# A macaron transformer block on one core: the engines' queues ordered by the scheduler's time-line machine

## The chip, the cores and the metric

The kernel runs on one core of a Trainium2 chip. Its time is that of the device in microseconds (us), given as the median over several runs. A core has a matrix engine (TensorE, PE in the profile), whose weight loads are listed apart (PEld), a vector engine (VectorE, DVE), a scalar engine (ScalarE, ACT), GpSimd (POOL) and SyncE (SP), which here issues nearly all DMAs. Each engine works through its own queue of instructions in a fixed order. An instruction waits at the head of its queue for semaphores that other engines or DMAs raise, and everything behind it on that engine waits with it.

## The reference

One layer on x of shape (1, 1024, 1024) with a condition c, all in float32:

```
h = x + 0.5 * g1 * postRMS(SwiGLU_1(mod1(preRMS(x))))
h = h + g2 * postRMS(Mixer(mod2(preRMS(h))))
h = h + 0.5 * g3 * postRMS(SwiGLU_2(mod3(preRMS(h))))

SwiGLU(u) = (silu(u @ w_gate) * (u @ w_up)) @ w_down      # 1024 -> 2816 -> 1024
stick-breaking (8 heads of 64): w[t,s] = sigmoid(z) * prod over s<j<t of sigmoid(-z[t,j]), s < t;  out = w @ v
differential (4 heads): (softmax(q1 k1 + bias) - lam * softmax(q2 k2 + bias)) @ v, normalised
Mixer = (sigmoid(ga) * (ya @ w_branch_sb) + sigmoid(gd) * (yd @ w_branch_da)) @ w_out
```

The scale and shift of mod1 to mod3 and the gates g1 to g3 come from c by a matrix-vector product with w_ada (adaLN): nine vectors of 1024 numbers.

## The kernel before

**Products.** A float32 product is made of three float32r products of 128 x 128 by 512 columns: each operand is split into a high half H (a cast, mostly on ScalarE: L141, L225, L960) and a low half L (a subtraction, mostly on VectorE: L142, L226, L961), and H x H, L x H and H x L are summed in one PSUM bank. Weights and activations come in as 128 x 1024 or 128 x 512 blocks over SP's queue (raw, raw2, stg), are split into wsH and wsL (or sbH, sbL, tbH, tbL), and TensorE works on them.

**Stages in order.** The *start*: the first adaLN vectors and the normalised, transposed and split input (uH, uL). *FFN 1, first part*: 11 pairs of gate and up matrices by a Strassen-like scheme (L298 to L300: blocks u, T1 to T4, B22, with weight sums s21 and s34 made on VectorE, L331 to L336; bank evictions into q on ScalarE and VectorE, L352 to L404). Between the pairs, the generator `steps` makes the adaLN vectors that later stages need, some instructions at a time: `mod_acc` (L82 to L91) loads a block of w_ada (wada, 512 KB, L87) and adds it to macc on VectorE, eight times per vector, in tiles of the tag "row", of which there are four; L101 and L125 bring macc through TensorE, and L126 and L127 make a gate row. *FFN 1, second part*: the down projection in seven phases p0 to p6 (L583 to L585, banks A and B, 11 blocks c each), the norm and residual (`finish`), and the transpositions of the mixer's input (L187, `tps<-ident,y`); in p6 the transpositions of the first four row blocks y0 to y3 meet the products of `h` = 0. *The mixer*: the projections of Q, K, V and the gates are "jobs" whose products are handed out one by one as filler (L813, L815, L817: pps, vps) between the instructions of attention. Units 0 to 3 are stick-breaking, two heads each, units 4 to 7 differential. In a stick-breaking step, TensorE makes z (L938, L939, L1005), ScalarE two sigmoids (L1006, L1007), VectorE a scan (L1010) and a product (L1011), TensorE transposes the weights be (L955, L956: trp), ScalarE casts tH (L960, L963, L965), VectorE subtracts tL (L961, L964, L966), and TensorE multiplies with v (L1021: pav). *The merge* multiplies the branches and gates, then comes *FFN 2* (no adaLN steps) and the output.

The filler around attention stands in the program like this (in `av`, cut): the next transposition, two filler products, then the products with the tiles of the transposition before.

```
for g in range(j + 1):
    tH, tL = nxt
    if g < j:
        nxt = transpose(g + 1)
    fill(2)
    ...  # two products with tH, two with tL
```

**What sets the order.** The program above is not the queue order. The tile framework's scheduler takes the instructions by a heap: of those that are ready, the one that stands first in the program goes out next. What is ready, and when an engine is free, it learns by letting the instructions run on a machine of its own that models the engines; the tiles of a pool are given out on the same machine. `TileContext` takes this machine's default. A few places are held by hand: `keep_in_program_order` in the start (L725) and `issue_after` in the mixer and the down projection.

## Time and profile before

| | us |
|---|---|
| median of 3 runs (2280.88 to 2286.59) | 2282.25 |
| span of the profiled execution | 2278.7 |
| TensorE busy | 2189.4 |
| VectorE busy | 1566.4 |
| ScalarE busy | 1043.7 |
| GpSimd busy | 70.0 |

The profiled execution was made apart from the three timed runs; its span, 2278.7 us, is the one time that there is for it, 0.2% below the median. A busy share is an average: a line such as "[1.62 <-DVE tL L961]" behind an instruction in the timeline says that its engine stood idle for 1.62 us before it and what ended the wait, and the windows give the same idle time by stage as the length less PE's busy time. Matrix instructions overlap (a record of a 512-column product lasts about 0.39 us while the next starts 0.23 us after it). Names are those of the program, without numbers in the profile (pav, tL, wsL) and with a running number in the order (pav_6879).

### The profile page before, as it was taken

To read this page: it belongs to the slowest core of one execution; us is meant where nothing else is said; L and a number is where in the kernel's file an instruction comes from. 1 tells how busy PE (TensorE), PEld (TensorE's weight loads), DVE (VectorE), ACT (ScalarE), POOL (GpSimd) and SP (SyncE) were. 2 spreads that over 40 slices of the span, in tenths; PEclk is the share of its full clock that TensorE was granted. 3 is DMA by queue.
4 is the path that set the end of the run, shared out by engine and by line. 5 is a ranking of instruction groups with operands and counts; after the bars stand their busy time and mean duration, and the time that the engine had idled before them with its cause. 6 is when DMAs were issued, how large, how long until landed. Compare 5 with 4: busy or idle time off the path is not lost.

```text
span 2278.7 us, 28622 instructions
## 1 busy us (share of the span) xinstructions
PE 2189.4 (96%) x10420; PEld 1792.8 (79%) x10420; DVE 1566.4 (69%) x2612; ACT 1043.7 (46%) x1882; POOL 70.0 (3%) x90
## 2 busy tenths in 40 slices
PE   5999999999999999999999999999999999999998
PEld 3787778878887877878888888788888787787786
DVE  6887876567577687576677577655885666755566
ACT  4633323325465555454454455554733232334454
POOL 1000000000000010011001010000000000000000
PEclk9999999999999999999999999999999999999999
DMA  7274874449786111110211122754474553537666
GB/s 305 85 271 169 292 254 170 145 154 316 246 284 216 62 32 45 38 48 30 62 56 63 48 87 75 248 192 130 153 250 171 178 173 128 189 115 260 217 220 219
DMA packets 137678, 364.38 MB, mean 160 GB/s; under 512 B 16705, under 2 KB 20801, under 8 KB 137537
## 3 DMA queue, kind: packets, MB, share of 16 engines
q1 hardware_dynamic: 135904, 356.79, 46.2%
q0 software_dynamic: 1632, 5.77, 0.7%
q8 instruction: 81, 1.33, 0.2%
q14 instruction: 61, 0.49, 0.1%
HBM read 272.32 MB, written 90.18 MB: 159 GB/s over the span
## 4 chain that ended last, share of the span: by engine, by line
PE 66%; DVE 17%; DMA 10%; ACT 5%; issue 2%; SPq 0%; DVEq 0%; ACTq 0%
PE bank L300 9%; PE bank L298 9%; PE bank L299 9%; PE pps L815 4%; PE pps L813 4%; DMA stg<-d_T 4%; PE pps L817 4%; DVE f L1010 2%; PE bankA L585 2%; PE bankA L584 2%; PE bankA L583 2%; DMA wada<-in_wada 2%; PE vps L813 1%; PE vps L817 1%; PE vps L815 1%
## 5 line engine op out<-in xcount | busy, mean ns | idle before, releaser
L813 PE MATMUL pps<-uH,wsH 128*128 128x512 f32 x512 | 209.7, 410 | 0.0
L815 PE MATMUL pps<-uL,wsH 128*128 128x512 f32 x512 | 205.3, 401 | 0.0
L817 PE MATMUL pps<-uH,wsL 128*128 128x512 f32 x512 | 204.6, 400 | 0.0
L226 DVE TENSOR_TENSOR tbL<-stg,tbH 128x512 fp32r<-128x512 f32 x154 | 105.8, 689 | 107.8 <-ACT tbH L225 107.2
L225 ACT CAST tbH<-stg 128x512 fp32r<-128x512 f32 x154 | 95.6, 621 | 156.1 <-DMA stg<-d_T 114.0
L298 PE MATMUL bank<-uH,wsH 128*128 128x512 f32 x352 | 142.1, 406 | 6.2 <-DVE uH L180 2.9
L584 PE MATMUL bankA<-tbL,sbH 128*128 128x512 f32 x352 | 138.5, 393 | 6.1 <-DVE tbL L226 5.9
L299 PE MATMUL bank<-uL,wsH 128*128 128x512 f32 x352 | 140.6, 400 | 1.5 <-POOL uL L181 1.5
L300 PE MATMUL bank<-uH,wsL 128*128 128x512 f32 x352 | 139.5, 397 | 0.0
L583 PE MATMUL bankA<-tbH,sbH 128*128 128x512 f32 x352 | 138.3, 394 | 0.4 <-ACT sbH L225 0.4
L585 PE MATMUL bankA<-tbH,sbL 128*128 128x512 f32 x352 | 138.4, 393 | 0.1
L142 DVE TENSOR_TENSOR wsL<-raw,wsH 128x1024 fp32r<-128x1024 f32 x72 | 88.0, 1222 | 70.4 <-ACT wsH L141 69.0
L226 DVE TENSOR_TENSOR sbL<-stg,sbH 128x512 fp32r<-128x512 f32 (+1 forms) x176 | 108.0, 619 | 33.2 <-ACT sbH L225 32.6
L225 ACT CAST wsH<-s 128x1024 fp32r<-128x1024 f32 x88 | 91.9, 1050 | 70.5 <-DVE s L332 48.7
L225 ACT CAST sbH<-stg 128x512 fp32r<-128x512 f32 (+1 forms) x176 | 98.1, 564 | 55.2 <-DMA stg<-hd_A 40.4
L365 ACT COPY q<-bank 128x512 f32<-128x512 f32 x44 | 25.8, 587 | 212.4 <-PE bank L300 212.4
L817 PEld LDWEIGHTS pps<-uH,wsL 128*128 128x128 f32 x512 | 96.9, 189 | 17.9
L226 DVE TENSOR_TENSOR wsL<-s,wsH 128x1024 fp32r<-128x1024 f32 x88 | 107.2, 1219 | 4.4 <-ACT wsH L225 4.0
L225 ACT CAST wsH<-raw 128x1024 fp32r<-128x1024 f32 (+1 forms) x88 | 73.2, 834 | 78.7 <-PE bank L299 44.8
L813 PEld LDWEIGHTS pps<-uH,wsH 128*128 128x128 f32 x512 | 97.6, 191 | 14.7
L815 PEld LDWEIGHTS pps<-uL,wsH 128*128 128x128 f32 x512 | 97.2, 190 | 14.6
L583 PE MATMUL bankB<-tbH,sbH 128*128 128x512 f32 x264 | 102.9, 390 | 0.1
(247 smaller groups left out, 5953.7 us busy)
## 6 DMA issues: line engine op xcount, KB each, us to landing
wada<-in_wada SPq DMA_DIRECT2D x56, 512.0 KB, 5.2
raw<-in_wg SPq DMA_DIRECT2D x50, 512.0 KB, 6.5
raw<-in_wu SPq DMA_DIRECT2D x50, 512.0 KB, 4.5
raw<-in_wd SPq DMA_DIRECT2D x44, 512.0 KB, 4.5
stg<-hd_A SPq DMA_DIRECT2D x88, 256.0 KB, 4.5
stg<-d_S SPq DMA_DIRECT2D x88, 256.0 KB, 3.6
stg<-d_T SPq DMA_DIRECT2D x88, 256.0 KB, 3.9
d_S<-s SPq DMA_DIRECT2D x40, 512.0 KB, 2.7
```

The lines of the kernel that those rows point to most:

```text
L142: eng.tensor_sub(l, raw, h.bitcast(F32))
L225: ACT.copy(h, src)
L226: V.tensor_sub(l, src, h.bitcast(F32))
L298: PE.matmul(ps, H[:, ks], bH, start=first and k == 0, stop=False, skip_group_check=not first)
L299: PE.matmul(ps, H[:, ks], bL, start=False, stop=False, skip_group_check=not first)
L300: PE.matmul(ps, L[:, ks], bH, start=False, stop=k == 3, skip_group_check=not first)
L583: PE.matmul(ps, sH[:, ts], tH, start=first, stop=False, skip_group_check=not check)
L584: PE.matmul(ps, sH[:, ts], tL, start=False, stop=False, skip_group_check=not check)
L585: PE.matmul(ps, sL[:, ts], tH, start=False, stop=last, skip_group_check=not check)
L813: PE.matmul(ps, aH, bH, start=i == 0, stop=False)
L815: PE.matmul(ps, aH, bL, start=False, stop=False)
L817: PE.matmul(ps, aL, bH, start=False, stop=i == n - 1)
```

## The change

One argument is added: the context's scheduler uses its other machine, the one named for a time line. No computation changes.

```diff
-    with tile.TileContext(nc) as tc:
+    with tile.TileContext(nc, schedule_with_timeline_sim=True) as tc:
         with ExitStack() as ctx:
             build(ctx, tc, A, o)
```

All engines have the same instructions before and after. At another place in its queue stand 6840 of 10416 on TensorE (2960 of them by more than 20 places, the largest 331 earlier and 136 later), 1880 of 2614 on VectorE (up to 72 earlier, 26 later), 1013 of 1770 on ScalarE, 509 of 960 on SP and none on GpSimd.

**TensorE, mixer, unit 0.** trp_6880 is one group of transposed weights, tH_6885 and tL_6886 its halves, tH_6836 and tL_6837 those of the group before, pav_6879 the output; pps are projection products. Before:

```order
L956 MATMUL trp_6880<-ident_69,be_6775 128x128
L815 MATMUL pps_6811<-uL5_1_6390,wsH_6670 128x512
L817 MATMUL pps_6811<-uH5_1_6389,wsL_6671 128x512
L813 MATMUL pps_6811<-uH6_1_6415,wsH_6670 128x512
L815 MATMUL pps_6811<-uL6_1_6416,wsH_6670 128x512
L817 MATMUL pps_6811<-uH6_1_6415,wsL_6671 128x512
L1021 MATMUL pav_6879<-tH_6836,v_6258 128x256 x2
L1021 MATMUL pav_6879<-tL_6837,v_6258 128x256 x2
...
L817 MATMUL pps_6811<-uH7_1_6438,wsL_6671 128x512
L813 MATMUL pps_6923<-uH0_0_5647,wsH_6676 128x512
L1021 MATMUL pav_6879<-tH_6885,v_6258 128x256 x2
L1021 MATMUL pav_6879<-tL_6886,v_6258 128x256 x2
```

After:

```order
L956 MATMUL trp_6880<-ident_69,be_6775 128x128
L813 MATMUL pps_6923<-uH6_0_5713,wsH_6676 128x512
L815 MATMUL pps_6923<-uL6_0_5714,wsH_6676 128x512
L817 MATMUL pps_6923<-uH6_0_5713,wsL_6677 128x512
...
L815 MATMUL pps_7038<-uL3_1_6341,wsH_6676 128x512
L817 MATMUL pps_7038<-uH3_1_6340,wsL_6677 128x512
L955 MATMUL trp_6898<-ident_69,be_6755 128x128
...
L813 MATMUL pps_7038<-uH5_1_6389,wsH_6676 128x512
L1021 MATMUL pav_6879<-tH_6836,v_6258 128x256 x2
L1021 MATMUL pav_6879<-tL_6837,v_6258 128x256 x2
L1021 MATMUL pav_6879<-tH_6885,v_6258 128x256 x2
L1021 MATMUL pav_6879<-tL_6886,v_6258 128x256 x2
```

Between the last transposition of trp_6880 and the first product with tL_6886 stand nine pps products before (five in the first piece, two that the dots leave out, two in the second) and 22 after; the four products with v stand together. Attention stands behind more projection products than before. At the ends of six of the steps of units 0 to 3, the products that stand ahead of it in the queue number 304 before and 334 after, 510 and 592, 606 and 728, 906 and 1008, 1132 and 1152, 1200 and 1255; in units 4 to 7 there are 0 to 71 more, and none more at the end.

**VectorE, FFN 1.** macc are the adaLN accumulations; q are evictions of banks and their sums, s21 and s34 weight sums, wsL splits. From the eviction q_1604 on, before:

```order
L371 TENSOR_TENSOR q_1604<-bank2_1606,q_1604 128x512
L355 TENSOR_TENSOR q_1463<-q_1604,q_1463 128x512
L226 TENSOR_TENSOR wsL_1754<-raw_1751,wsH_1753 128x1024
L399 TENSOR_TENSOR q_1668<-bank_1591,q_1668 128x512
L355 TENSOR_TENSOR q_1527<-q_1668,q_1527 128x512
L404 TENSOR_TENSOR q_1653<-bank2_1655,q_1653 128x512
L355 TENSOR_TENSOR q_1512<-q_1653,q_1512 128x512
L467 TENSOR_TENSOR s21_1711<-q_1512,q_1527 128x512
L469 TENSOR_TENSOR s34_1712<-q_1463,q_1512 128x512
```

After, from the same instruction on:

```order
L371 TENSOR_TENSOR q_1604<-bank2_1606,q_1604 128x512
L91 SCALAR_TENSOR_TENSOR macc_1744<-wada_2051,csil_78,macc_1744 128x1024
L226 TENSOR_TENSOR wsL_1754<-raw_1751,wsH_1753 128x1024
L355 TENSOR_TENSOR q_1463<-q_1604,q_1463 128x512
L91 SCALAR_TENSOR_TENSOR macc_1744<-wada_2054,csil_78,macc_1744 128x1024
L91 SCALAR_TENSOR_TENSOR macc_1744<-wada_2057,csil_78,macc_1744 128x1024
L91 SCALAR_TENSOR_TENSOR macc_1744<-wada_2060,csil_78,macc_1744 128x1024
L399 TENSOR_TENSOR q_1668<-bank_1591,q_1668 128x512
L91 SCALAR_TENSOR_TENSOR macc_1744<-wada_2346,csil_78,macc_1744 128x1024
L355 TENSOR_TENSOR q_1527<-q_1668,q_1527 128x512
L89 TENSOR_SCALAR macc_2360<-wada_2361,csil_78 128x1024
L91 SCALAR_TENSOR_TENSOR macc_2360<-wada_2364,csil_78,macc_2360 128x1024
```

Accumulations stand between the evictions; the steps on wada_2051 to wada_2364 stood 38 to 68 rows further on before. Up to the split of wsL_1949 there are 14 accumulations from here, where there were three and three gate-row instructions (L126, L127). TensorE's instructions in this stretch keep their order but for the first products of a next matrix, which stand 12 to 48 rows earlier. On SP, the loads of these wada tiles, 14 of them, now stand ahead of the weight loads raw_1906 and raw2_1942, as the macc order needs them.

**TensorE, FFN 1, phase p6.** tps are transpositions of the row blocks y0 to y3, bankA_3878 and bankA_3879 the two banks of `h` = 0. Before, the transpositions of y3 follow the first six products:

```order
L187 MATMUL tps_5673<-ident_69,y2_3872 128x128
L583 MATMUL bankA_3878<-tbH_5749,sbH_5743 128x512
L584 MATMUL bankA_3878<-tbL_5750,sbH_5743 128x512
L585 MATMUL bankA_3878<-tbH_5749,sbL_5744 128x512
L583 MATMUL bankA_3879<-tbH_5749,sbH_5743 128x512
L584 MATMUL bankA_3879<-tbL_5750,sbH_5743 128x512
L585 MATMUL bankA_3879<-tbH_5749,sbL_5744 128x512
L187 MATMUL tps_5640<-ident_69,y3_3873 128x128
```

After, 38 products stand ahead of them (the dots leave out 30 of them):

```order
L187 MATMUL tps_5673<-ident_69,y2_3872 128x128
L583 MATMUL bankA_3878<-tbH_5749,sbH_5743 128x512
L584 MATMUL bankA_3878<-tbL_5750,sbH_5743 128x512
L585 MATMUL bankA_3878<-tbH_5749,sbL_5744 128x512
L583 MATMUL bankA_3878<-tbH_5767,sbH_5761 128x512
...
L585 MATMUL bankA_3878<-tbH_5839,sbL_5834 128x512
L585 MATMUL bankA_3879<-tbH_5839,sbL_5834 128x512
L583 MATMUL bankA_3878<-tbH_5857,sbH_5851 128x512
L583 MATMUL bankA_3879<-tbH_5857,sbH_5851 128x512
L187 MATMUL tps_5640<-ident_69,y3_3873 128x128
```

The transpositions of y0 to y2 stand at the same place; those of y3 moved behind the products of blocks c = 0 to 5 and two of the next.

## The prediction

> **What bounds the kernel now.** I read the page first: its engine line and its chain of waits.
>
> ```profile
> PE 2189.4 (96%) x10420; PEld 1792.8 (79%) x10420; DVE 1566.4 (69%) x2612; ACT 1043.7 (46%) x1882; POOL 70.0 (3%) x90
> PE 66%; DVE 17%; DMA 10%; ACT 5%; issue 2%; SPq 0%; DVEq 0%; ACTq 0%
> ```
>
> TensorE is busy for 96% of the span, and the work is the same before and after, so an order can win only what PE idles, 2278.7 − 2189.4 = 89 us, and what it loses at a lower clock; it can lose without such a limit. Next I cut the span into stages with the windows view (after the window: its length, busy time and instructions of PE, PEld, DVE, ACT and POOL, the granted clock, the DMA share, GB/s).
>
> ```profile
> 0.00:75.00 75.00, 42.62 (x165) 30.81 (x166) 50.32 (x89) 37.40 (x60) 9.79 (x12) 0.86 0.61 239
> ...
> 228.00:399.00 171.00, 167.06 (x730) 133.57 (x729) 132.63 (x174) 53.81 (x75) 0.00 (x0) 1.00 0.69 239
> ...
> 684.00:741.00 57.00, 51.31 (x233) 41.53 (x232) 40.31 (x77) 32.19 (x69) 0.00 (x0) 0.94 0.65 216
> 741.00:798.00 57.00, 54.06 (x347) 48.01 (x346) 35.97 (x64) 29.30 (x57) 5.33 (x8) 0.97 0.19 59
> 798.00:1083.00 285.00, 269.96 (x1549) 225.87 (x1548) 202.30 (x283) 152.48 (x346) 29.15 (x32) 0.99 0.12 38
> 1083.00:1140.00 57.00, 52.74 (x330) 46.56 (x329) 36.33 (x65) 28.15 (x60) 0.00 (x0) 0.94 0.20 62
> 1140.00:1425.00 285.00, 282.99 (x1560) 242.04 (x1559) 205.28 (x630) 145.04 (x316) 17.98 (x24) 1.00 0.20 66
> 1425.00:1767.00 342.00, 339.82 (x1500) 273.96 (x1499) 240.91 (x335) 176.62 (x268) 0.00 (x0) 1.00 0.57 190
> 1767.00:1824.00 57.00, 54.33 (x226) 42.76 (x225) 38.93 (x56) 16.83 (x23) 0.00 (x0) 0.97 0.53 180
> ...
> 2223.00:2280.00 57.00, 44.92 (x196) 36.20 (x194) 34.33 (x63) 23.36 (x55) 0.00 (x0) 0.94 0.62 211
> ```
>
> PE's idle time by stage is length less busy time: start 75 − 42.62 = 32.4; FFN 1 from 228 to 399, 3.9; the boundary of FFN 1 and the mixer, 5.7 at clock 0.94; the mixer 2.9 + 15.0 + 4.3 + 2.0 = 24.3; 1767 to 1824, 2.7; the tail 12. The mixer's stick-breaking half (798 to 1083) is the largest piece outside the start.
>
> **The mixer, the main term.** Of the groups by line, these two show what it waits for, and the timeline shows one such wait.
>
> ```profile
> L1021 PE MATMUL pav<-tL,v 128*128 128x256 f32 (+1 forms) x160 | 36.8, 299 | 12.6 <-DVE tL L961 10.6 <-DVE tL L966 1.8
> L961 DVE TENSOR_TENSOR tL<-trp,tH 128x512 fp32r<-128x512 f32 x72 | 49.3, 686 | 17.0 <-ACT tH L960 16.3
> ```
>
> ```profile
> 806.75 0.27 PE L956 MATMUL trp<-ident,be 128*128 128x128 f32 x1
> ...
> 808.86 2.28 DVE L1010 TENSOR_TENSOR_SCAN f<-f 128x1024 f32<-128x1024 f32 x1
> ...
> 809.30 0.39 PE L817 MATMUL pps<-uH,wsL 128*128 128x512 f32 x1
> ...
> 809.53 0.39 PE L813 MATMUL pps<-uH,wsH 128*128 128x512 f32 x1
> ...
> 811.06 0.67 DVE L961 TENSOR_TENSOR tL<-trp,tH 128x512 fp32r<-128x512 f32 x1
> ...
> 811.78 0.51 PE L1021 MATMUL pav<-tL,v 128*128 128x256 f32 x2 [1.62 <-DVE tL L961]
> ```
>
> The last transposition starts at 806.75. Its low half tL is made behind a 2.28-us scan on VectorE's queue and is ready at 811.06 + 0.67 = 811.73, that is 5.0 us later. PE has in between only what the order put there: projection products, 0.23 us apart (809.30 to 809.53), and a few short ones, together 3.4 us; then it stands for 1.62 us. In the order of before (front part, PE in unit 0) nine projection products lie between the transpositions of trp_6880 and the use of tL_6886; the new order has 22. At 0.23 us each, and the short ones at their traced time, the cover goes from 3.4 to 7.3 us against the 5.0 needed. The same sum over all 120 first uses of a tL tile: median 4.5 before, 6.5 after, and 38 covers under 4 us become 15. VectorE's order at this place hardly changes.
>
> A long wait costs more than itself:
>
> ```profile
> 972.34 0.33 PE L1021 MATMUL pav<-tH,v 128*128 128x128 f32 x1 [1.91 <-ACT tH L965]
> 966.90:976.20 9.30, 7.39 (x33) 5.92 (x31) 7.11 (x10) 3.64 (x9) 0.00 (x0) 0.82 0.18 63
> ```
>
> Behind the 1.91-us wait, the granted clock over 9.3 us is 0.82, so 0.18 x 9.3 = 1.7 us are lost besides. The Trainium skill (TensorE: Matmul & The Clock Gate, section "Why this matters for your kernels") asks only that there be no idle gaps over about 3 us between bursts; by it this gap would cost no clock and the stage's sum would be 1.7 us smaller. The trace disagrees, and the row decides.
>
> At stake from 798 to 1083: 15.0 + 1.7 = 16.7 us. If the waits went in step with the short covers, 15/38 would stay and 16.7 x 23/38 = 10.1 would go; if the longer cover ended every wait, all 16.7. I take 13, in the middle. The 4.3 us idle and 0.06 x 57 = 3.4 us of clock from 1083 to 1140 I leave: there attention, which the new order lets lag behind the projections by up to 122 products, has caught up most of this (20 to 55 products). Mixer: **−13, from −17 to −5** (the low end of the gain: half of the 10.1).
>
> **FFN 1: adaLN steps moved ahead.** Each step is one VectorE accumulation (L89, L91) behind its own 512-KB load.
>
> ```profile
> L91 DVE SCALAR_TENSOR_TENSOR macc<-wada,csil,macc 128x1024 f32<-128x1024 f32 x49 | 62.8, 1281 | 11.4 <-DMA wada<-in_wada 11.2
> wada<-in_wada SPq DMA_DIRECT2D x56, 512.0 KB, 5.2
> ```
>
> ```profile
> 202.65 0.69 DVE L371 TENSOR_TENSOR q<-bank,q 128x512 f32<-128x512 f32 x1 [4.37 <-PE bank L300]
> ...
> 211.04 0.69 DVE L399 TENSOR_TENSOR q<-bank,q 128x512 f32<-128x512 f32 x1 [5.84 <-PE bank L300]
> ...
> 213.77 0.69 DVE L404 TENSOR_TENSOR q<-bank,q 128x512 f32<-128x512 f32 x1 [1.31 <-PE bank L300]
> ...
> 217.04 0.68 DVE L355 TENSOR_TENSOR q<-bank,q 128x512 f32<-128x512 f32 x1
> 217.64 0.68 DVE L126 TENSOR_TENSOR grow<-gps,br 128x512 f32<-128x512 f32 x1
> ...
> 223.02 1.22 DVE L226 TENSOR_TENSOR wsL<-s,wsH 128x1024 fp32r<-128x1024 f32 x1
> ...
> 229.57 1.28 DVE L91 SCALAR_TENSOR_TENSOR macc<-wada,csil,macc 128x1024 f32<-128x1024 f32 x1
> 230.77 0.68 DVE L497 TENSOR_TENSOR t<-raw,t 128x512 f32<-128x512 f32 x1
> ...
> 242.06 0.69 DVE L331 TENSOR_TENSOR s<-raw 128x512 f32<-128x512 f32 x1 [4.93 <-DMA raw<-in_wu]
> ...
> 245.71 1.21 DVE L226 TENSOR_TENSOR wsL<-s,wsH 128x1024 fp32r<-128x1024 f32 x1
> ```
>
> VectorE idles 4.37 + 5.84 + 1.31 us before the three evictions at 202.65, 211.04 and 213.77. The new order fills just these places. Instructions start 0.60 us apart for 512 columns (217.04 to 217.64) and 1.20 for an accumulation (229.57 to 230.77). Worked from 202.65: the eviction, four accumulations, a split and an add take 2 x 0.60 + 5 x 1.20 = 7.2 and end at 209.9, ahead of the 211.04 at which PE gives the next bank. From there two rows of 512 columns and three accumulations (4.8) bring the third eviction to 215.8 in place of 213.8; twelve more rows of 512 and three more accumulations (10.8) bring the split of wsL_1794, at 223.02 before, to 226.6. It is 3.6 us late, and before it had no time to spare: it ended at 224.24, and PE's first product with it started at 224.30.
>
> ```profile
> 224.30 0.50 PE L300 MATMUL bank<-T2H,wsL 128*128 128x512 f32 x1
> ```
>
> So PE may stand for 3.6 us here. Until the next such split (245.71 before) the queue catches up: fifteen rows of 512 and seven of 1024 columns, four accumulations among them, take 17.4 and bring it to 244.0, in the idle time that the wait for the raw load (4.93 us before 242.06) left. That wait stays.
>
> Each accumulation also needs its load. SP's queue now has 14 wada loads ahead of two weight loads; with four buffers a step can come every (5.2 + 1.28)/4 = 1.6 us. The DMA engines are free enough here (198 to 217, below).
>
> ```profile
> 198.00:217.00 19.00, 19.00 (x83) 15.24 (x82) 7.34 (x11) 2.87 (x5) 0.00 (x0) 1.00 0.16 56
> ```
>
> I count +3, most of the 3.6. Lower bound: the 3.9 idle from 228 to 399 goes with the accumulations that leave this stretch, −4. Upper: with nothing hidden, 14 accumulations ahead of the split at 245.71 (16.8) in place of three and three row operations (6.0) would be +11; I end at 8 and keep the rest for a rival. FFN 1: **+3, −4 to +8**.
>
> **The boundary of FFN 1 and the mixer.**
>
> ```profile
> 692.62 2.25 PE L187 MATMUL tps<-ident,y 128*128 128x128 f32 x10 [3.61 <-DVE y L172]
> ...
> 698.55 0.66 PE L187 MATMUL tps<-ident,y 128*128 128x128 f32 x4 [1.62 <-DVE y L172]
> ...
> 703.38 0.66 PE L187 MATMUL tps<-ident,y 128*128 128x128 f32 x4 [0.47 <-ACT u L178]
> ```
>
> The first wait stays: the transpositions of y0 to y2 stand where they stood. Those of y3 now stand behind 38 products in place of 6: at 0.23 us, 8.7 us of cover from the end of the first wait's transpositions (692.62 + 2.25 = 694.9), so they come up at 703.6, well behind the 698.55 at which y3 was ready. So 1.62 + 0.47 go, and likely one of the two stretches at a lower clock that the row of 684 to 741 holds (0.06 x 57 = 3.4 us lost, 1.7 as behind the wait above): 3.8 at stake, **−3, −5 to +1**; above nothing if the loads of the products now put first are late.
>
> **The rest.** Start: VectorE fills its waits otherwise, the weight loads of block 2 go out later; from its rows I can't tell a sign, **+1, −2 to +4**. The merge holds no wait that moves. FFN 2 has no adaLN steps and keeps its 2.7 us (1767 to 1824) (**0, −3 to +3**), and so has the tail.
>
> **Sum.** +1 + 3 − 3 − 13 = −12 against the profiled span: 2278.7 → 2266.7. The span is 3.6 us (0.2%) under the median of the runs, 2282.25, so the time is 2270.
>
> **The rivals.**
>
> *The waits only move (chance 0.20).* The products that now cover the first units' attention are missing later: by the last stick-breaking units the lag falls from 122 to 20 products. For it: VectorE is at 202.30 of 285 where it waits least for work, so attention itself can't run much faster. Then mixer and boundary give back their 16 and the start's and FFN's +4 stay or are hidden: 2282 to 2286, no change within 0.3%, about what a measurement of this kernel can tell (2275.4 to 2289.1). Against: in units 4 to 7 the median cover of the transpositions is 9.7 us before and 10.6 after, by the same sum.
>
> *Slower by the adaLN queue (0.13).* If loads do not keep up, accumulations stand at the head of VectorE's in-order queue, and the splits and evictions behind them wait; PE waits for these. Price: 10.8 of work put ahead, 14 x (1.6 − 1.2) = 5.6 of load pace, +4 in the start, and 1.7 of clock behind each of four gaps, 6.8: 27 us in place of 4. With −16 elsewhere it is +11: 2293. It decides from 23 us on (the −16 and the 0.3%). For: L91 already waits 11.2 us for its loads. Against: 4.37 + 5.84 + 1.31 us of VectorE's idle time at just these places.
>
> *Slower by the catch-up (0.05).* Between two steps in which attention catches up 82 products (906 to 1132 issued), 82 x 0.23 = 19 us of cover are missing; with VectorE as the bound all of it shows, with clock for four gaps 6.8: −12 + 26 = +14, 2296. Against: 0.71 of VectorE's time is busy, and 19 us less in that stretch still fits.
>
> *The clock falls under the new interleaving (0.03).* Products now change bank more often. At the lowest rate the mixer shows, 0.94, six windows of 57 us lose 6 x 3.4 = 20 us: 2270 + 20 = 2290. The rows speak against: 1140 to 1425 rotates through the same pools of banks at clock 1.00. The Trainium skill (TensorE: Matmul & The Clock Gate, section "A second HAM failure mode: psum-queue depth-cycling") holds that cycling through banks makes PE micro-idle and its clock swing.
>
> *The flag changes nothing (0).* The order rows exclude it: 6840 of PE's rows stand elsewhere.
>
> **How the numbers follow.** My forecast has the other 0.59. The terms' bounds add to −19 and +23 about the sum, in squares to −9 and +11; as they fall neither all together nor quite apart I go halfway, −14 and +17: 2256 to 2287. To it come the rivals up to 2293, about half of the slow ones (0.09) beyond it, while 0.03 lie under 2256. Range 2256 to 2293. Faster by over 0.3% (under 2275.4): the forecast without its upper end, 0.55. Slower (over 2289.1): 0.13 + 0.05 and 0.01 of the clock's: 0.19. Same: the rest, 0.26.
>
> **What would show it.** Right: from 798 to 1083 PE idle about 3 to 5 us in place of 15, pav's wait for tL under 5 us of 12.6; a single wait at 689, none at 697; FFN 1 from 217 to 243 with a wait of up to 3 us on wsL or bank. Wrong: L91's wait for wada over 20 us with PE idle beside it from 200 to 270; PE idle after 1083 over 15 us; or a clock under 0.97 where PE hardly idles.

## The result and the profile after

The changed kernel takes 2338.01 us (median of 4 runs, 2336.31 to 2340.83) against 2282.26 for the kernel before (4 runs): ratio 1.0249, 95% interval 1.0234 to 1.0265. It is slower by 56 us, where the prediction had 2270 and a range up to 2293. The profiled execution has a span of 2334.5 us against 2278.7, a difference of 55.8, and these 55.8 us are what is explained below.

The page's engine line and chain of waits, after:

```profile
PE 2208.7 (95%) x10420; PEld 1808.2 (77%) x10420; DVE 1564.4 (67%) x2612; ACT 1038.0 (44%) x1882; POOL 63.3 (3%) x90
PE 70%; DVE 15%; DMA 7%; issue 2%; ACT 2%; SPq 0%; DVEq 0%; ACTq 0%
```

TensorE idles 2334.5 − 2208.7 = 125.8 us, 36.5 more than before. But it is also *busy* 19.3 us longer, with the same 10420 instructions: the mean granted clock was 0.977 against 0.989. So about two thirds of the loss are waits and one third is, in the main, the lower clock.

The windows view, cut at the first instruction of a stage on TensorE. In the FFNs each row of the one kernel holds the same work as the row of the other. In the mixer it doesn't quite: the row of units 0 to 3 holds 58 TensorE instructions more after than before, and the row of units 4 to 7 holds 58 fewer, since projection products were done earlier. Before: FFN 1's middle and late pairs, the mixer's units 0 to 3, its units 4 to 7, FFN 2's pairs, FFN 2's down projection.

```profile
138.00:301.00 163.00, 160.75 (x694) 128.35 (x692) 123.57 (x162) 50.48 (x70) 0.00 (x0) 1.00 0.66 233
301.00:503.00 202.00, 199.92 (x862) 159.82 (x862) 135.19 (x186) 67.60 (x95) 2.31 (x4) 1.00 0.51 176
...
734.00:1122.00 388.00, 365.77 (x2103) 308.23 (x2102) 273.06 (x406) 209.58 (x461) 34.48 (x40) 0.98 0.15 47
1122.00:1425.00 303.00, 300.99 (x1710) 260.04 (x1709) 210.43 (x639) 149.51 (x325) 17.98 (x24) 1.00 0.20 64
...
1609.50:2053.00 443.50, 439.75 (x1902) 352.65 (x1900) 305.64 (x428) 167.93 (x244) 2.17 (x4) 1.00 0.49 169
```

The same five, after:

```profile
145.00:329.00 184.00, 166.89 (x693) 131.23 (x692) 129.18 (x167) 50.53 (x71) 0.00 (x0) 0.95 0.66 221
329.00:539.50 210.50, 201.79 (x862) 159.13 (x861) 127.40 (x178) 66.96 (x95) 2.31 (x4) 1.00 0.43 144
...
771.00:1153.00 382.00, 369.80 (x2161) 318.24 (x2161) 269.17 (x409) 208.21 (x463) 28.39 (x40) 0.97 0.16 49
1153.00:1459.00 306.00, 298.39 (x1652) 257.86 (x1652) 210.01 (x636) 146.41 (x322) 16.84 (x24) 0.98 0.19 62
...
1642.00:2105.00 463.00, 446.44 (x1902) 354.04 (x1901) 306.40 (x427) 167.54 (x244) 2.17 (x4) 0.99 0.47 162
```

The first number behind the window is its length. By stage, with the rest of the cuts:

| stage | before, us | after, us | difference |
|---|---|---|---|
| start and first pairs | 138 | 145 | +7 |
| FFN 1, middle pairs | 163 | 184 | +21 |
| FFN 1, late pairs | 202 | 210.5 | +8.5 |
| FFN 1, down projection and boundary | 231 | 231.5 | +0.5 |
| mixer, to the last stick-breaking product | 388 | 382 | −6 |
| mixer, the rest | 303 | 306 | +3 |
| merge | 184.5 | 183 | −1.5 |
| FFN 2, pairs | 443.5 | 463 | +19.5 |
| FFN 2, down projection and output | 225.7 | 229.5 | +4 |

So the loss is in the two FFNs, in the pairs of gate and up matrices, and the mixer, the main term of the prediction, gives back 3 us where 13 were expected. (Of its two rows only this sum is like for like.) What TensorE waits for in the pairs, before and then after, from the groups by line:

```profile
L298 PE MATMUL bank<-T2H,wsH 128*128 128x512 f32 x176 | 70.0, 398 | 2.1 <-ACT wsH L225 2.1
```

```profile
L298 PE MATMUL bank<-T2H,wsH 128*128 128x512 f32 x176 | 73.7, 420 | 24.3 <-ACT wsH L225 24.3
L300 PE MATMUL bank<-T2H,wsL 128*128 128x512 f32 x176 | 73.2, 416 | 8.9 <-DVE wsL L226 8.9
```

The product with T2 is a matrix's first one that needs weight *sums* (s21). Its wait for the cast of that sum grew from 2.1 to 24.3 us. One such place in FFN 2, after, in the timeline (start, duration, engine, line, operation; idle time before it in brackets):

```profile
1852.03 0.69 DVE L404 TENSOR_TENSOR q<-bank,q 128x512 f32<-128x512 f32 x1 [1.31 <-PE bank L300]
1857.10 0.68 DVE L332 TENSOR_TENSOR s<-s,raw 128x512 f32<-128x512 f32 x1
...
1857.87 1.04 ACT L225 CAST wsH<-s 128x1024 fp32r<-128x1024 f32 x1 [4.79 <-DVE s L332]
...
1855.08 0.40 PE L298 MATMUL bank<-uH,wsH 128*128 128x512 f32 x1
...
1857.62 0.39 PE L300 MATMUL bank<-uH,wsL 128*128 128x512 f32 x1
1858.97 0.50 PE L298 MATMUL bank<-T2H,wsH 128*128 128x512 f32 x1 [0.96 <-ACT wsH L225]
...
1860.77 0.50 PE L300 MATMUL bank<-T2H,wsL 128*128 128x512 f32 x1 [0.61 <-DVE wsL L226]
```

And the same place before:

```profile
1813.18 0.69 DVE L404 TENSOR_TENSOR q<-bank,q 128x512 f32<-128x512 f32 x1 [1.31 <-PE bank L300]
1818.25 0.68 DVE L332 TENSOR_TENSOR s<-s,raw 128x512 f32<-128x512 f32 x1
...
1819.20 2.08 ACT L225 CAST wsH<-s 128x1024 fp32r<-128x1024 f32 x2
...
1812.76 0.39 PE L300 MATMUL bank<-B22H,wsL 128*128 128x512 f32 x1
1815.78 0.39 PE L298 MATMUL bank<-uH,wsH 128*128 128x512 f32 x1
...
1821.24 0.40 PE L298 MATMUL bank<-T2H,wsH 128*128 128x512 f32 x1
```

VectorE needs the same time in both: from the eviction at L404, which the end of the B22 products releases, to the sum at L332 it is 5.07 us, and the cast is ready 6.9 us after the eviction began (1858.91 − 1852.03). What differs is TensorE's cover, that is, the products that it can work on while that chain runs. Before, 36 products stand between the last B22 product and the T2 product (12 of T4, 24 of the next matrix's u), 36 x 0.23 = 8.3 us. After, ten of the first twelve u products were already taken, ahead of T3 and B22: 26 x 0.23 = 6.0 us are left, and TensorE waits 0.96 for the high and 0.61 for the low half. This pair of waits comes eight times in FFN 2: 12.6 of its 19.5 us. The window of the pairs has 6.7 us more of busy time besides (446.44 − 439.75).

### The profile page after: what moved, and what is told of

The parts are those of the page before. It is cut to its first block, busy times and chain, and to the rows that moved or that the text cites. A ratio compares the mean times of both kernels' runs of the same rounds, so it can differ in the third digit from the quotient of the medians.

```text
span 2334.5 us, 28716 instructions
## 1 busy us (share of the span) xinstructions
PE 2208.7 (95%) x10420; PEld 1808.2 (77%) x10420; DVE 1564.4 (67%) x2612; ACT 1038.0 (44%) x1882; POOL 63.3 (3%) x90
## 4 chain that ended last, share of the span: by engine, by line
PE 70%; DVE 15%; DMA 7%; issue 2%; ACT 2%; SPq 0%; DVEq 0%; ACTq 0%
PE bank L300 9%; PE bank L298 9%; PE bank L299 8%; PE pps L813 5%; PE pps L817 5%; PE pps L815 5%; PE bankA L583 2%; PE bankA L584 2%; PE bankA L585 2%; PE bankB L583 2%; PE bankB L585 2%; PE bankB L584 2%; DMA stg<-d_T 2%; DVE wsL L226 1%; PE pav L1021 1%
## 5 line engine op out<-in xcount | busy, mean ns | idle before, releaser
L298 PE MATMUL bank<-uH,wsH 128*128 128x512 f32 x352 | 142.0, 405 | 8.2 <-ACT wsH L225 2.6
L300 PE MATMUL bank<-uH,wsL 128*128 128x512 f32 x352 | 140.3, 399 | 0.8 <-DVE wsL L226 0.8
L583 PE MATMUL bankA<-tbH,sbH 128*128 128x512 f32 x352 | 127.1, 397 | 6.6 <-ACT tbH L225 4.1
L813 PEld LDWEIGHTS pps<-uH,wsH 128*128 128x128 f32 x512 | 98.0, 191 | 19.3 <-ACT wsH L141 0.7
L399 DVE TENSOR_TENSOR q<-bank,q 128x512 f32<-128x512 f32 x44 | 30.2, 687 | 122.7 <-PE bank L300 114.6
L226 DVE TENSOR_TENSOR wsL<-raw,wsH 128x1024 fp32r<-128x1024 f32 (+1 forms) x88 | 83.9, 954 | 39.3 <-ACT wsH L225 39.3
```

Source lines behind the costliest of these rows:

```text
L226: V.tensor_sub(l, src, h.bitcast(F32))
L298: PE.matmul(ps, H[:, ks], bH, start=first and k == 0, stop=False, skip_group_check=not first)
L300: PE.matmul(ps, L[:, ks], bH, start=False, stop=k == 3, skip_group_check=not first)
L583: PE.matmul(ps, sH[:, ts], tH, start=first, stop=False, skip_group_check=not check)
L813: PE.matmul(ps, aH, bH, start=i == 0, stop=False)
```

## The experiments

The two queue orders are both known, so an experiment can take one stage's or one engine's order from the one kernel and leave the rest to the other. Rows are chained by order-only edges (no wait for completion), in the kernel before:

```diff
+def force(tc, nc, order):
+    by = {i.name: i for i in nc.cur_bb.bb.instructions}
+    dep = mybir.DependencyInfo(mybir.DependencyClass.NoSync, mybir.DependencyReason.DATA)
+    for names in order:
+        for a, b in zip(names, names[1:]):
+            tc.add_manual_dep(by[f"I-{b}"], f"I-{a}", dep, reason="order")
...
             build(ctx, tc, A, o)
+            force(tc, nc, ORDER)
```

ORDER lists, for each engine, the rows that are forced, in their new order; it is said with each run. Ratios are to the kernel before on the same chip (2282 to 2283 us), with 95% intervals.

**One stage at a time.** ORDER holds all five engines' rows of FFN 1 and its boundary, or of mixer and merge, or of FFN 2, as in the changed kernel.

> The start, FFN 1 and the boundary (all five engines) in the changed kernel's order, everything from the mixer on in the order of before. Theory (each stage pays for its own order, and the stages add): the changed trace reaches the mixer's first projection at 771.3 us against 734.1, so +37 us, 2319. Rival (FFN 1's loss is made good later, or part of it comes only together with the new mixer): under +30, below 2312. The prediction's step had +1 for all of this stretch, 2283.

Measured: 2320.4 us, ratio 1.0160 (1.0143 to 1.0178).

> Only the mixer and the merge (all five engines) in the changed kernel's order, the rest as before. Theory (the mixer itself gains little): from the first projection to FFN 2's first product the changed trace takes 870.8 us against 875.4, so -4.6 us, 2278. Rival (the mixer's order gains the predicted 13 us, and what comes over from FFN 1 or SP's queue takes it away in the changed kernel): -10 to -13, 2269 to 2272.

Measured: 2276.3 us, ratio 0.9968 (0.9952 to 0.9984).

> Only FFN 2 and the output (all five engines) in the changed kernel's order. Theory: from FFN 2's first product to the end the changed trace takes 692.4 us against 669.2, so +23 us, 2305; the T2 products wait for the cast of the weight sums, 0.96 and 0.61 us in nearly every pair of matrices. Rival (FFN 2 suffers from a mixer that ends otherwise): under +12, below 2294. The prediction had 0 here.

Measured: 2306.0 us, ratio 1.0097 (1.0081 to 1.0114).

+37.2, −6.9 and +22.8 add to +53.1, and the whole change is +55.7 by the medians: within what the runs scatter the stages add, and none is seen to suffer from another. The mixer alone does make the kernel faster, by half of what was predicted.

**FFN 2: TensorE's order or VectorE's?** First, in the changed kernel, the first products with u of each next matrix are held back:

```diff
-            product(self.bank, self.w["A11"], lambda k: first_half("B11", k), True, (0, 1))
+            product(self.bank, self.w["A11"], lambda k: first_half("B11", k), True, (0, 1), pin=True)
...
-            PE.matmul(ps, H[:, ks], bH, start=first and k == 0, stop=False, skip_group_check=not first)
+            p = PE.matmul(ps, H[:, ks], bH, start=first and k == 0, stop=False, skip_group_check=not first)
+            if pin and k == 0:
+                tc.keep_in_program_order(p)
```

> The changed kernel, but the first product of each next matrix in FFN 1 and FFN 2 is held behind the products of the matrix before on TensorE's queue. Theory (taken ahead of the T4 products, that first product no longer covers the sums, casts and splits that the T2 products wait for): the waits of 0.96 and 0.61 us go in both FFNs, FFN 2 loses 17 to 20 us of its +23, FFN 1 another 8 to 12, so 2338 - 25 to - 32 = 2306 to 2313. Rival (the sums are late by VectorE's own order or by late weight loads, and TensorE's order is only a sign of it): the waits stay, at most -8, 2330 to 2338.

Measured: 2322.1 us, ratio 1.0170 (1.0154 to 1.0185): −16, between the two. By its trace, FFN 2's pairs fell from +19.5 to +9.6, but FFN 1 only from +37 to +34. The hold takes back only a part of TensorE's order: up to twelve products with T2 still stand ahead of the B22 products that they followed before. Then the opposite, in the kernel before: ORDER holds TensorE's queue alone, from FFN 2 on.

> The kernel before, with TensorE's queue alone in the changed order from FFN 2 on; the other engines' queues are made by the default machine around it. Theory (the early first products alone make the T2 products wait): 9 pairs x 1.57 us, less what the hold took away (10) as the lower bound: +10 to +16, 2293 to 2299. Rival (VectorE's and ScalarE's new order is needed for it): under +4, below 2287.

Measured: 2304.1 us, ratio 1.0097 (1.0081 to 1.0113): +22, more than the theory's bound and all that FFN 2's whole order costs. Its timeline has the same wait at the same distances:

```profile
1824.05 0.69 DVE L404 TENSOR_TENSOR q<-bank,q 128x512 f32<-128x512 f32 x1 [1.31 <-PE bank L300]
1829.12 0.69 DVE L332 TENSOR_TENSOR s<-s,raw 128x512 f32<-128x512 f32 x1
...
1830.99 0.50 PE L298 MATMUL bank<-T2H,wsH 128*128 128x512 f32 x1 [0.96 <-ACT wsH L225]
```

5.07 us from L404 to L332 again, and the 0.96 again. VectorE's rows were not forced here; the default machine put them around TensorE's, so they don't stand quite as before either, but the chain takes the same time and the cover is the shorter one. So TensorE's order is enough for FFN 2's loss. The last run on the FFNs, below, has the converse.

**FFN 1: early products, bunched accumulations, or both?** TensorE's bank products alone, in the kernel before (ORDER: the rows of L298 to L300 in FFN 1):

> The kernel before, with the bank products (L298 to L300) of FFN 1 alone in the changed kernel's TensorE order; adaLN and the other engines as the default machine puts them around it. Theory (without the cover of the first product, accumulations cost wherever they stand): with adaLN back in its old places FFN 1 still lost 30 us, so +15 to +28, 2298 to 2311. Rival (the early products cost only together with the accumulations that are bunched ahead): at most +8, below 2292.

Measured: 2326.6 us, ratio 1.0193 (1.0179 to 1.0207): +44, beyond both bounds. Eleven of it come in the start, where the forced rows meet other ones than in the changed kernel; from the first pairs on it is 30 us, where the whole change lost 38. But the run doesn't part the two suspects, since the default machine took accumulations early here too: ahead of the 36th bank eviction on VectorE (rows q<-bank) stand 25 of them, 15 in the kernel before and 30 in the changed one. The other suspect, first by putting VectorE's adaLN rows back (ORDER: all of FFN 1 in the changed order, but on VectorE the adaLN rows at their old places, and those of TensorE and SP left free):

> As the run with FFN 1 alone in the changed order (2320), but VectorE's adaLN instructions (L89, L91, L126, L127) stand where they stood before among the other rows, and their loads and TensorE rows follow them. Theory (accumulations put ahead of evictions and weight sums hold TensorE): the losses of 8 us from 98 to 138 and of 19 us from 200 to 301 go, the waits per pair stay: -22 to -28, 2292 to 2298. Rival (accumulations only fill VectorE's idle time, as my prediction's step had it, and the stretch is slow by the early first products): at most -5, over 2315.

Measured: 2321.9 us, ratio 1.0164 (1.0144 to 1.0184): no gain over the 2320.4. The theory falls as it stood, and the time is the rival's. This is the run that answers for TensorE: the accumulations stand as before (15 ahead of the 36th bank eviction), and the pairs still lose 30 us, where the whole change lost 37. At the point where the changed order had lost 28 us (329) this one has lost 13.7, so the accumulations that no longer stood there had cost 14. From there to the end of the pairs it loses 16 where the changed order lost 8, and 6 more in the down projection. The longest wait of that stretch stands over 140 us behind the last accumulation in it:

```profile
488.28 0.69 DVE L404 TENSOR_TENSOR q<-bank,q 128x512 f32<-128x512 f32 x1 [1.31 <-PE bank L300]
...
495.68 0.69 DVE L332 TENSOR_TENSOR s<-s,raw 128x512 f32<-128x512 f32 x1
...
497.55 0.80 PE L298 MATMUL bank<-T2H,wsH 128*128 128x512 f32 x1 [3.29 <-ACT wsH L225]
```

Three gate-row instructions (L126 twice, L127) stand at their old place in this chain, which takes 7.40 us in place of 5.07, and the wait is 3.29 in place of 0.96: longer by the same 2.33 us. In the kernel before the chain at this place took 7.40 us as well (459.41 to 466.81), and TensorE went on to T2 at 469.19 without a wait. With the cover shortened, adaLN's rows cost at their old places too. And in the changed kernel, with the scheduler left to place them late:

```diff
-                V.tensor_scalar_mul(acc, w, csil[:, 0:1])
+                p = V.tensor_scalar_mul(acc, w, csil[:, 0:1])
             else:
-                V.scalar_tensor_tensor(acc, w, csil[:, k:k + 1], acc, ALU.mult, ALU.add)
+                p = V.scalar_tensor_tensor(acc, w, csil[:, k:k + 1], acc, ALU.mult, ALU.add)
+            tc.keep_in_program_order(p)
```

> The changed kernel, but each accumulation of adaLN is held behind the VectorE instructions that stand ahead of it in the program, so it isn't taken early. Theory: as above, 2338 - 22 to - 28 = 2310 to 2316, L91 waits less for wada, FFN 2 loses about what it lost. Rival (VectorE was idle there anyway): 2333 to 2340.

Measured: 2342.3 us, ratio 1.0248 (1.0221 to 1.0274): no gain, 2 us above the rival's range (the four runs lie from 2333 to 2348). Both holds together:

> The changed kernel with both holds: the first product of a next matrix on TensorE, and the accumulations on VectorE. Theory (two separate costs that add): 2338 - 16 (measured for the first hold alone) - 25 = 2295 to 2302. Rival (one cost seen twice: the T2 products wait because accumulations delay the sums): no better than the better of the two alone, 2310 or more.

Measured: 2308.7 us, ratio 1.0106 (1.0089 to 1.0123). Neither theory: singly the two holds gave −16 and +4, together −29. FFN 1 lost 20 us instead of 34 or 32. That is what two causes give when either alone is enough to keep TensorE waiting. The 20 us that stay are no proof of a third cause, since both holds are partial: the T2 products stay early, and the accumulations stand later than before (12 ahead of the 36th bank eviction in place of 15). Whether the bunched accumulations are enough by themselves was the open point, tried in the kernel before (ORDER: on VectorE L89, L91 and the evictions L371, L399, L404 of FFN 1 as in the changed kernel; on TensorE the bank products as before):

> The kernel before, with FFN 1's adaLN accumulations (L89, L91) among the bank evictions (L371, L399, L404) on VectorE as in the changed kernel; TensorE's bank products are held in their old order, so nothing is taken early there. Theory (either cause alone is enough): the bunched accumulations hold evictions and sums, +15 to +30, 2297 to 2312. Rival (they cost only where the early products have taken the cover): at most +5, below 2288. My prediction's step for this had +3.

Measured: 2344.9 us, ratio 1.0283 (1.0260 to 1.0305): +62, over twice the theory's upper bound. Its first long wait on VectorE and what TensorE lost by it:

```profile
121.39 2.61 DVE L91 SCALAR_TENSOR_TENSOR macc<-wada,csil,macc 128x1024 f32<-128x1024 f32 x2 [3.13 <-DMA wada<-in_wada]
123.91 0.68 DVE L404 TENSOR_TENSOR q<-bank,q 128x512 f32<-128x512 f32 x1
...
124.65 0.79 PE L298 MATMUL bank<-T1H,wsH 128*128 128x512 f32 x1 [14.48 <-DVE q L404]
```

The eviction at L404 stands behind accumulations, these behind their loads, and TensorE needs the bank: 14.48 us. In the changed kernel the same eviction stands behind five accumulations, and TensorE waits 3.83 us:

```profile
111.70 1.28 DVE L91 SCALAR_TENSOR_TENSOR macc<-wada,csil,macc 128x1024 f32<-128x1024 f32 x1
...
113.61 1.28 DVE L91 SCALAR_TENSOR_TENSOR macc<-wada,csil,macc 128x1024 f32<-128x1024 f32 x1
114.81 0.68 DVE L404 TENSOR_TENSOR q<-bank,q 128x512 f32<-128x512 f32 x1
...
115.55 0.79 PE L298 MATMUL bank<-T1H,wsH 128*128 128x512 f32 x1 [3.83 <-DVE q L404]
```

The mechanism is the same; the size, 62, isn't the changed kernel's. Loads and other rows were left to the default machine here, which is the likely reason, but no run shows it. Last, in the changed kernel, exactly the bank products of both FFNs back in their old order:

> The changed kernel, with the bank products (L298 to L300) of both FFNs in TensorE's order of before; the mixer stays as changed. Theory (TensorE's early first products cost FFN 2 its 20 us, and FFN 1 where no accumulations are bunched): FFN 2 loses 5 to 8 in place of 20 and FFN 1 15 to 30 in place of 37: 2300 to 2318. Rival (with TensorE's old order all goes, since the hold used before moved more than these products): mixer's -5 and no loss, 2278 to 2288.

Measured: 2313.0 us, ratio 1.0140 (1.0123 to 1.0158), as the theory had it: by the trace FFN 2's pairs lose 4 in place of 19.5, FFN 1 27 in place of 37. With the run that forced TensorE's queue alone, this shows FFN 2's cause from both sides. In FFN 1 the accumulations are early here (26 ahead of the 36th bank eviction) and TensorE's products are not: 27 us. With the products early and the accumulations not, it was 30; with both, 37. Either is enough for most of the loss. The orders of the other queues changed in all three, so what share is theirs stays open.

**The mixer's two halves.** ORDER: units 0 to 3 on all engines as in the changed kernel, then what is left of the mixer (units 4 to 7 and the merge) in the old order; the complement; and the first with phase p6 of FFN 1 in the changed order besides.

> Only units 0 to 3 of the mixer in the changed kernel's order; what is left of the mixer and all else as before. With the whole mixer in the new order the stretch to the last stick-breaking product took 6.5 us less and the rest of the mixer 3.6 more. Theory (the loss after it is the missing filler, used up by the units before): the loss comes back whatever order the rest has, 2276 to 2279. Rival (the loss is in the differential units' own new order): -8 to -10, 2273 to 2275.

Measured: 2269.5 us, ratio 0.9932 (0.9915 to 0.9949). The theory of filler that is missing later falls: with 59 TensorE instructions fewer in it, the stretch of units 4 to 7 takes 295.8 us in place of 303.0, and TensorE idles 2.0 us in it, as before. In the changed kernel the same stretch, with 1652 TensorE instructions against 1651, takes 306.

> The complement of the run with units 0 to 3: these as before, and what is left of the mixer in the changed kernel's order. Theory (the differential units' own new order costs): whole mixer 2276.3 less units 0 to 3 alone 2269.5 is +6.8 us, so 2288 to 2291. Rival (it costs only after a first half that has used up the filler): no loss, 2281 to 2285.

Measured: 2288.6 us, ratio 1.0032 (1.0017 to 1.0047), as the theory had it. Units 4 to 7, with the merge, lose by their own new order: +6.4 alone, and 2276.3 − 2269.5 = 6.8 behind the new first half. The merge is not where it is lost (184.5 us before, 183 in the changed kernel).

> Units 0 to 3 of the mixer (2269.5 alone) and phase p6 of FFN 1's down projection in the changed kernel's order, all else as before. Theory (my prediction's step for p6 holds where the products it puts first are not late): the waits of 1.62 and 0.47 us at the transpositions of y3 go, -2 to -4, 2265 to 2268. Rival (the stretch ahead of the first wait gets longer by as much, as it did in the changed kernel, where the first wait was 4.29 and another 1.05 us): 2269 to 2271.

Measured: 2271.6 us, ratio 0.9951 (0.9938 to 0.9964), against 0.9932 without p6: nothing gained, the intervals overlap, and the time is the rival's but for half a microsecond. Units 0 to 3 in the changed order alone are the best version found, 13.9 us better than the kernel before on the same chip.

## Why the prediction was wrong, step by step

| step | predicted | measured |
|---|---|---|
| start | +1 | about −1 to the first pairs |
| FFN 1 | +3 (−4 to +8) | +38 to +39 |
| boundary of FFN 1 and mixer | −3 | about 0 |
| mixer | −13 (−17 to −5) | −3 |
| FFN 2 | 0 (−3 to +3) | +19.5 in the pairs, +4 behind them |

**FFN 2, "0": the step that failed by itself.** The text said "FFN 2 has no adaLN steps and keeps its 2.7 us". The front part names such row moves for FFN 1 ("the first products of a next matrix, which stand 12 to 48 rows earlier"); FFN 2 has them too, and no term of the sum priced them in either. They add no work and take no wait; they take *cover* from the chain L404, sums, cast, split, which ended 1.0 us ahead of need before in that place (cast of s21 ready at about 1820.2, used at 1821.24). The prediction measured cover in the mixer, where products moved in between, and did not where they moved out. The sentence was also false as it stood: FFN 2 has one adaLN vector (8 accumulations at L89 and L91 before 2052); its loss doesn't come from them, as the run with TensorE's queue alone shows.

**FFN 1, "+3".** The mechanism was named, as the rival with a chance of 0.13: accumulations at the head of VectorE's queue, ahead of evictions and splits. The working let them fill three idle stretches and found the queue 3.6 us late, because it took the loads as there in time ("a step can come every 1.6 us") and TensorE's gift of the next bank as fixed. After, the third eviction of that stretch starts at 231.69 in place of 213.77:

```profile
212.66 1.29 DVE L91 SCALAR_TENSOR_TENSOR macc<-wada,csil,macc 128x1024 f32<-128x1024 f32 x1 [1.79 <-DMA wada<-in_wada]
...
230.49 1.28 DVE L91 SCALAR_TENSOR_TENSOR macc<-wada,csil,macc 128x1024 f32<-128x1024 f32 x1 [2.69 <-DMA wada<-in_wada]
231.69 0.68 DVE L404 TENSOR_TENSOR q<-bank,q 128x512 f32<-128x512 f32 x1
```

13.6 of these 18 us are what TensorE was late already: the last of the B22 products, which release this eviction, ends at 227.3 in place of 213.7, and twelve products with u (2.8 us) were taken ahead of them. The other 4.4 are accumulations and their waits for loads. What TensorE lost by it follows at once, first for the bank, then for the cast of the sum:

```profile
232.43 0.50 PE L298 MATMUL bank<-uH,wsH 128*128 128x512 f32 x1 [2.31 <-DVE q L404]
...
241.49 0.80 PE L298 MATMUL bank<-T2H,wsH 128*128 128x512 f32 x1 [6.06 <-ACT wsH L225]
```

The rival's price, 27, was also short, since the early products add to it and the first pairs lose 7 us, 3.83 of them by the same mechanism, a stretch that the prediction did not read. The sign that was to show it, over 20 us of waiting for wada at L91, stayed out (13.7 us after, 11.2 before), so it was ill chosen.

**The mixer, "−13".** The waits that the term was made of did go:

```profile
L1021 PE MATMUL pav<-tL,v 128*128 128x256 f32 (+1 forms) x160 | 36.6, 294 | 1.0 <-DVE tL L966 1.0
L1021 PE MATMUL pav<-tH,v 128*128 128x256 f32 (+1 forms) x160 | 37.4, 293 | 4.5 <-DVE ysb L1026 4.5
L955 PE MATMUL trp<-ident,be 128*128 128x128 f32 x128 | 33.8, 280 | 3.5 <-DVE tL L961 3.5
L955 PE MATMUL trp<-ident,ex 128*128 128x128 f32 x64 | 17.1, 291 | 3.6 <-DVE r L1050 3.6
```

pav's wait for tL is 1.0 us in place of 12.6. New ones came: with all products of a step standing together behind its transpositions, the next step's first product waits until the one pav bank is read (ysb, 4.5), and a transposition for a trp bank (3.5); the third and fourth row are waits of units 0 to 3 and 4 to 7. To the last stick-breaking product 6 us were gained, 3 lost again after it. The rival "the waits only move" was right in the result, but its reason, filler that is missing later, was wrong: with the old order behind the new first half the stretch from the first projection to the merge is 12.8 us shorter (677.8 against 690.6), close to the 13 that were predicted. Only 8.0 of them are idle time (16.3 against 24.3) and 4.8 are busy time (661.6 against 666.4), while the term was made of idle time and clock from 798 to 1083, so the agreement is partly luck. The term had the right sign and waits for the half that it was read from, and it was silent on units 4 to 7. Most of the idle time that these add is the wait of the fourth row, 3.6 us, which is 0.4 before and 0.5 in the run that keeps their old order; which of their moved rows brings it was not tried.

**The boundary, "−3".** The transpositions of y3 no longer wait, as said; the first wait, which "stays", grew, and the first product behind it waits too:

```profile
731.14 2.39 PE L187 MATMUL tps<-ident,y 128*128 128x128 f32 x10 [4.29 <-DVE y L172]
...
734.59 0.77 PE L583 MATMUL bankA<-tbH,sbH 128*128 128x512 f32 x1 [1.05 <-DVE y L654]
```

4.29 + 1.05 = 5.3 us, against 3.61 + 1.62 + 0.47 = 5.7 before. The stretch at a lower clock that was to go grew instead: 10.2 us at half clock from 729.7, against twice 3.4 us before (from 692.8 and from 706.5). In the run with p6 added it brought nothing that could be measured; why the first wait grew was not tried.

**The clock.** The prediction allowed 1.7 us for each wait of about 2 us. TensorE was busy 19.3 us longer for the same work, about half of the added waits (36.5); a chance of 0.03 was given to a lower clock by bank changes. Where the changed kernel goes through the mixer's banks in the new order without a wait, the clock is 1.00 (the row below, units 0 to 3), so here it follows the waits and not the interleaving:

```profile
855.00:912.00 57.00, 57.00 (x320) 48.39 (x318) 43.65 (x63) 34.86 (x77) 8.53 (x12) 1.00 0.18 54
```

## What to carry to other kernels

When an order changes, price every group of rows that moved by the cover that it gives or takes: the work of the bottleneck engine between the end of a producer chain and its first use, at both the place it left and the place it went to. On a kernel that is 96% busy, small early starts of ready work can cost, since a chain that was just hidden (here 7 us under 8.3) shows at once and can pay again in clock. A schedule that is better in one stage and worse in others can be taken stage by stage: units 0 to 3 alone in the new order gave 0.7%.

## What the runs showed of the hardware that was not expected

A lower granted clock doesn't need a long wait. In the changed kernel the clock is at half for 13.7 us from 1118.8, where no wait is over 0.84 us, behind 6.8 us with 1.5 us idle in all and one wait of 1.04:

```profile
1118.80:1132.50 13.70, 11.55 (x33) 8.81 (x34) 11.30 (x12) 8.25 (x15) 0.00 (x0) 0.50 0.24 73
1112.00:1118.80 6.80, 5.27 (x35) 3.98 (x33) 6.77 (x10) 5.43 (x15) 0.00 (x0) 1.00 0.14 48
...
1116.68 0.45 PE L1021 MATMUL pav<-tH,v 128*128 128x256 f32 x2 [1.04 <-DVE ysb L1026]
1119.07 0.80 PE L938 MATMUL z<-kd,q 128*128 128x512 f32 x1 [0.76 <-ACT f L1007]
1128.29 0.79 PE L817 MATMUL pps<-uH,wsL 128*128 128x512 f32 x1 [0.84 <-DVE wsL L142]
```

While it is low, 512-column products start 0.43 us apart in place of 0.23 (the first behind a wait lasts 0.79 us), operands still come late, and the clock stays low through waits of 0.3 to 0.8 us. Nor does the same wait always bring it: the pair of 0.96 and 0.61 us comes eight times in FFN 2 of the changed kernel, and the clock falls to half, for 3.4 us, behind two of them (from 1944.8 and from 1989.2). In the 6.8 us ahead of 1118.8, ten of the TensorE instructions are transpositions; whether that has a part in it is not shown. The Trainium skill (TensorE: Matmul & The Clock Gate, section "A second HAM failure mode: psum-queue depth-cycling") says that frequent micro-idles between groups of products make the clock swing; these rows agree with it, though here the micro-idles are waits for VectorE and ScalarE and not a matter of banks. The same page's rule of no gaps over about 3 us (section "Why this matters for your kernels") is not enough here: this stretch keeps it and loses half its clock.
